# Half of a block's opening modulation as row products on the matrix engine, and attention maxima spread over the projections

## The chip, the cores and the metric

The kernel runs on one core of a Trainium2 chip. The time is the device time of one launch in microseconds, the median of several runs. The core's engines have queues of their own: TensorE (PE in the rows) multiplies, VectorE (DVE), ScalarE (ACT) and GpSimd (POOL) work element by element, and SyncE (SP) issues the transfers.

## What is computed

Two layers of a block with three mixers side by side (retention, latent attention, gated linear attention) on 1024 tokens of width 1024, all in fp32. Each layer is opened by a normalisation whose scale and shift come from a vector `c` (the modulation), and the projections of all mixers follow from its result:

```python
c_act = jax.nn.silu(c)
for l in range(DEPTH):
    shift, scale, gate = jnp.split(c_act @ ada_w[l] + ada_b[l], 3, axis=-1)
    h = rms_norm(x, norm_w[l]) * (1.0 + scale[:, None, :]) + shift[:, None, :]
    proj = h @ w_in[l]
    ...
    mixed = jnp.concatenate([r_o * jax.nn.silu(rz), m_o * jax.nn.silu(mz),
                             g_o * jax.nn.silu(gz)], axis=-1)
    x = x + gate[:, None, :] * (mixed @ w_out[l])
return rms_norm(x, final_norm)
```

`m_o` is softmax attention with 8 heads over 1024 queries and keys in causal blocks; its softmax subtracts a maximum of the scores, which the kernel has to find first.

## The kernel before

Everything is kept transposed: channels lie on the partitions, in 8 tiles of 128 channels by 1024 tokens, each in two halves of 512 tokens. Every product is made of three multiplications (`mm3`, L554 to L558): operands are split into a high part, rounded for the fast format, and a low part, and PE does high by high, high by low and low by high into one PSUM bank. The order on PE is the order in which the code is written; the other engines' orders are set by a scheduler that goes by estimated times, with some steps pinned.

**The opening** (`start`). Transfers are issued in order of need: the tiles of x, then for each of the 8 tiles the weights of the modulation, and between the first of them the weights of three projections (rq1, rq2, rk1). Modulation comes in columns of 128 channels: `column(k)` makes the scale of tile k as a product along the row on DVE (`along(1)`, L301: one pass over 1024 elements, the sum kept), and the shift on PE as 8 fp32 multiplications with one moving column each (L311) for the first `SHIFT_PE` = 5 columns, or by a second pass on DVE for the rest. `make(k)` makes tile k: scaling on DVE (L347), high part on ACT (L348), low part on DVE (L354), with the next column's work put between the two. Then `mm` multiplies tile k with each of three weights, 18 multiplications of 512 columns; the first three tiles defer some of them by the table `behind`, as the weights are split (`w_split`, a cast on ACT and a subtraction on DVE) only one by one.

**The maxima** (`mla_max`). For each head, eight query blocks of 128 are multiplied with all the keys that they see, up to 512 at a time (L1245, 12 multiplications a head, 96 a layer), and DVE reduces each (L1247). A head ends with a closing: a reduce over the blocks (L1213), a multiplication that turns the result round (L1217), a copy and a store. The function is a generator that runs as a task: `proj`, `proj_v` and others call `tick()` as they go, which counts every task down and runs it up to its next `yield`, whose number says how many ticks to pause. So `MAXW` = 1.15 ticks lie between two maxima, and a closing waits 7 ticks between its reduce and its multiplication, during which the head's other maxima wait too, as it is called inside with `yield from`. `drain(t)` runs a task to its end at once. In `layer` the task `big` starts before the projection gk, runs through gv (called pv in the rows), gz0, gz1, mz0 to mz3, and what is left of it is drained ahead of mv, the values of the latent attention, which starts in `mla_first` and `mla`. Also in these projections stand `next_chunk` calls: six pieces of modulation for this layer and the next, each 8 passes over 512 elements on DVE (L576), with pieces at c, g, k, n and so on (`CHUNKS`), and an addition (L579).

`self.maxp` names the PSUM pools that the maxima rotate through; two banks at a time.

Of the kernel before, what the change touches and what calls it, by code (L numbers as in the profile page):

```python
# [16 lines left out]
D = 1024  # L17
DEPTH = 2
# [17 lines left out]
SHIFT_PE = 5  # L36
MAXW = 1.15
# [77 lines left out]
def host_layout(x, c, positions, norm_w, ada_w, ada_b, w_in, mla_q_norm, w_uq, mla_kv_norm,  # L115
# [20 lines left out]
    A["aws"] = ada_w[0][:, :128 * SHIFT_PE].reshape(KT, 128, SHIFT_PE, 128).transpose(2, 1, 0, 3).reshape(SHIFT_PE, 128, D)  # L136
# [5 lines left out]
    def col(v):  # L142
# [5 lines left out]
        c[0].reshape(KT, 128).T], 1)  # L148
# [8 lines left out]
for _n, _w in (("normw", DEPTH * 8), ("adab", DEPTH * 24), ("qn", DEPTH * 2), ("kvn", DEPTH),  # L157
               ("gb2", DEPTH), ("gln", DEPTH), ("fin", 8), ("inv", 1), ("c", 8)):
    VO[_n] = _o
    _o += _w  # L160


class Builder:
# [55 lines left out]
    def start(self):  # L219
# [24 lines left out]
        for k in range(KT):  # L244
            if k < len(names):
                wst[names[k]] = self.sl(name="wst")
                dma(wst[names[k]], A["wi"][0, MIDX[names[k]]])
            aw[k] = [self.sl(name="aw") for _ in range(2)]
            dma(aw[k][1], A["awc"][2 + k // 4, k % 4])
            dma(aw[k][0], A["aws"][k] if k < SHIFT_PE else A["awc"][k // 4, k % 4])  # L250
# [10 lines left out]
        self.silu(self.silc, self.vec[:, o:o + KT], self.sm([128, KT]), self.sm([128, KT]))  # L261
        ab = self.sm([128, KT])
# [30 lines left out]
        def column(k):  # L293


            self.lab = "ada_"
            ch, j = k // 4, slice(k % 4, k % 4 + 1)
            t = self.sm([128, 2])

            def along(i):  # L300
                V.scalar_tensor_tensor(aw[k][i], aw[k][i], 1.0, self.silrow, ALU.mult, ALU.mult,  # L301
                                       accum_out=t[:, i:i + 1])
            along(1)
            o = VO["normw"] + k
            V.scalar_tensor_tensor(self.mod[0][2 + ch][:, j], t[:, 1:2], ab[:, k:k + 1], self.vec[:, o:o + 1],
                                   ALU.add, ALU.mult)
            src = t[:, 0:1]
            if k < SHIFT_PE:
                ps = self.ps()
                for i in range(KT):  # L310
                    nc.tensor.matmul(ps[:, 0:1], aw[k][0][:, 128 * i:128 * i + 128], self.silc[:, i:i + 1],  # L311
                                     start=(i == 0), stop=(i == KT - 1))
                src = ps[:, 0:1]
            else:
                along(0)
            o = VO["adab"] + k
            nc.scalar.activation(self.mod[0][ch][:, j], src, AF.Identity, bias=self.vec[:, o:o + 1])
        w_split("rq1")
# [19 lines left out]
        def make(k):  # L338
# [10 lines left out]
            if 0 < k < KT - 1:  # L349
                column(k + 1)  # L350
# [4 lines left out]
            if k == 0:  # L355
                column(1)
            return last
        behind = {0: (("rq1", 0),), 1: (("rq1", 1), ("rq2", 0), ("rq2", 1)),
                  2: (("rq1", 2), ("rq2", 2), ("rk1", 0), ("rk1", 1), ("rk1", 2))}
        for k in range(KT):  # L360
            self.start_last = make(k)
            if k < 2:
                w_split(names[k + 1])
            for n, i in behind.get(k, [(n, k) for n in names]):
                mm(n, i)
            if k == 2:
                self.trig(ang, kk, s)
# [827 lines left out]
    def mla_max(self, l):  # L1195
# [14 lines left out]
        def close(h, mx):  # L1210
# [3 lines left out]
            yield 7  # L1214
# [9 lines left out]
        for h in range(MH):  # L1224
            yield MAXW
# [6 lines left out]
            for i in range(8):  # L1232
                n = 128 * (i + 1)
                for j in range((n + 511) // 512):
                    if i or j:
                        yield MAXW
                    if i == 2 and done:
                        yield from close(*done)
                        done = None
                        yield MAXW  # L1240
# [228 lines left out]
    def layer(self, l, src):  # L1469
# [3 lines left out]
        self.maxp = ("mm", "s")  # L1473
# [48 lines left out]
        for i in range(2):  # L1522
            mixed[6 + i] = self.proj_silu(l, f"gz{i}")
            self.next_chunk("jk"[i])
        mz = [self.proj_silu(l, "mz0")]
# [63 lines left out]
```

## Time and profile before

| | |
|---|---|
| median of 3 runs | 1185.25 us (1184.59 to 1190.17) |
| the profiled execution | 1184.63 us, its span 1182.8 us |
| mean granted clock of PE | 0.977 of full speed |
| PE, DVE, ACT, POOL busy | 95%, 67%, 50%, 45% of the span |
| chain that ended last | PE 75%, DVE 12%, ACT 4%, DMA 4% |
| moved by DMA | 169 MB, mean 143 GB/s |

The profile is one execution on the chip. Busy time of an engine is that of its instructions; a matmul's end is modelled, so neighbouring ones overlap in their rows. The granted clock says at what share of 2.4 GHz the chip let PE run; 0.50 is 1.2 GHz. In a row of a timeline the first number is its start in us, the second its length, then engine, line, operation, names of the tiles (result, then operands), partitions and elements, and "x16" for a run of 16 records; brackets say how long the engine had waited just before and for whom.

### The profile page before, as it was taken

What the parts mean: (1) busy time and instruction counts of PE and PEld (TensorE: products, weight loads), DVE (VectorE), ACT (ScalarE), POOL (GpSimd) and SP (SyncE); (2) the same over time, 40 slices, a digit from 0 to 9 for tenths busy, and PEclk for the clock granted to TensorE, in tenths of its full rate; (3) what the DMA queues carried; (4) which work ended last, traced back from release to release, by engine and by line L of the source; (5) the groups of instructions that cost most, each with busy time, mean ns of one, the idle gap of its engine ahead of it and who ended that gap; (6) DMA issues with size and microseconds to landing.
All of it is one profiled execution on the core that took longest, in us unless ns stands there. A gap on an engine that the chain in (4) does not pass through costs nothing.

```text
span 1182.8 us, 16979 instructions
## 1 busy us (share of the span) xinstructions
PE 1128.0 (95%) x5968; PEld 942.6 (80%) x5968; DVE 796.7 (67%) x1366; ACT 596.6 (50%) x1164; POOL 529.5 (45%) x459
## 2 busy tenths in 40 slices
PE   6999999998999899999999999999899999999996
PEld 4878977787878688887887898778788868888896
DVE  7866595686675656768875476666675666686754
ACT  6434334433545578853543434434256447886431
POOL 0064153643443346673555333444553334668620
PEclk8899999998999899999999999999999989999998
DMA  9816563651136434248453356355111653424722
GB/s 370 296 48 194 170 225 133 187 170 41 42 120 201 119 90 108 64 152 302 169 183 99 99 172 238 99 184 157 41 41 41 195 134 90 108 63 163 249 88 72
DMA packets 65585, 169.01 MB, mean 143 GB/s; under 512 B 10262, under 2 KB 13334, under 8 KB 65500
## 3 DMA queue, kind: packets, MB, share of 16 engines
q1 hardware_dynamic: 65500, 167.93, 44.7%
q8 instruction: 47, 0.77, 0.3%
q14 instruction: 38, 0.31, 0.1%
HBM read 125.36 MB, written 38.41 MB: 138 GB/s over the span
## 4 chain that ended last, share of the span: by engine, by line
PE 75%; DVE 12%; ACT 4%; DMA 4%; issue 3%; POOL 1%; SPq 0%; DVEq 0%; ACTq 0%; POOLq 0%
PE mhead_psacc L1296 3%; PE mhead_psacc L1294 3%; PE mhead_psacc L1295 3%; PE wo_pspj L558 2%; PE wo_pspj L556 2%; PE wo_pspj L557 2%; PE pmz_pspj L556 2%; PE wo_pss L557 2%; PE wo_pss L556 2%; PE wo_pss L558 2%; PE pmz_pspj L557 2%; PE pmz_pspj L558 2%; DVE mmax_mx L1247 2%; PE mhead_pss L1263 2%; PE mhead_pss L1262 2%
## 5 line engine op out<-in xcount | busy, mean ns | idle before, releaser
L457 POOL TENSOR_TENSOR wwo_wl<-wwo_wst,wwo_wh 128x1024 fp32r<-128x1024 f32 x27 | 69.0, 2559 | 40.6 <-ACT wwo_wh L456 40.5
L1271 POOL TENSOR_TENSOR mhead_wh<-mhead_p,mhead_wh 128x384 fp32r<-128x384 f32 (+1 forms) x48 | 58.1, 1211 | 56.7 <-DVE mhead_wh L1270 56.7
L1247 DVE TENSOR_REDUCE mmax_mx<-mmax_psmm 128x1 f32<-128x512 f32 (+1 forms) x96 | 57.3, 596 | 26.4 <-PE mmax_psmm L1245 25.6
L576 DVE SCALAR_TENSOR_TENSOR ada_aw<-ada_aw,silrow 128x512 f32<-128x512 f32 x64 | 62.0, 986 | 18.5 <-DMA ada_aw<-awc 18.2
L1276 DVE TENSOR_TENSOR mhead_ph<-mhead_pss,mhead_ph 128x512 fp32r<-128x512 f32 x48 | 33.1, 689 | 38.6 <-ACT mhead_pss L1275 38.6
L556 PE MATMUL pmz_pspj<-mkh_h,wmz_wh 128*128 128x512 f32 x128 | 52.5, 410 | 0.0
L1271 POOL TENSOR_TENSOR mhead_wl<-mhead_p,mhead_wl 128x128 fp32r<-128x128 f32 (+1 forms) x48 | 35.8, 746 | 34.1 <-DVE mhead_wl L1270 34.1
L557 PE MATMUL pmz_pspj<-mkh_h,wmz_wh 128*128 128x512 f32 x128 | 50.3, 393 | 0.0
L558 PE MATMUL pmz_pspj<-mkh_h,wmz_wl 128*128 128x512 f32 x128 | 50.1, 392 | 0.0
L558 PE MATMUL wo_pspj<-gran_mx,wwo_wl 128*128 128x512 f32 (+1 forms) x120 | 44.8, 374 | 1.7 <-POOL wwo_wl L457 1.7
L556 PE MATMUL wo_pspj<-gran_mx,wwo_wh 128*128 128x512 f32 (+1 forms) x120 | 45.3, 377 | 0.2 <-ACT wwo_wh L456 0.2
L1245 PE MATMUL mmax_psmm<-mmax_mxk,mmax_mxq 104*128 104x512 f32 (+1 forms) x96 | 38.9, 408 | 6.6 <-DVE mmax_mx L1247 5.9
L557 PE MATMUL wo_pspj<-gran_mx,wwo_wh 128*128 128x512 f32 (+1 forms) x120 | 44.8, 373 | 0.0
L556 PE MATMUL wo_pss<-gran_mx,wwo_wh 128*128 128x512 f32 (+1 forms) x120 | 44.6, 371 | 0.0
L558 PE MATMUL wo_pss<-gran_mx,wwo_wl 128*128 128x512 f32 (+1 forms) x120 | 44.1, 368 | 0.0
L557 PE MATMUL wo_pss<-gran_mx,wwo_wh 128*128 128x512 f32 (+1 forms) x120 | 44.1, 368 | 0.0
L600 ACT ACTIVATE ssq_sq<-ssq_x 128x512 f32<-128x512 f32 (+1 forms) x31 | 16.5, 534 | 51.7 <-DVE ssq_x L1373 51.7
L457 POOL TENSOR_TENSOR wrk_wl<-wrk_wst,wrk_wh 128x1024 fp32r<-128x1024 f32 x3 | 8.1, 2688 | 76.0 <-ACT wrk_wh L456 76.0
L1247 DVE TENSOR_REDUCE mmax_mx<-mmax_pss 128x1 f32<-128x256 f32 (+2 forms) x72 | 36.5, 507 | 7.5 <-PE mmax_pss L1245 6.8
L605 DVE TENSOR_TENSOR ssq_sq<-ssq_sq,ssq_sq 128x512 f32<-128x512 f32 (+1 forms) x30 | 30.5, 1017 | 14.0 <-ACT ssq_sq L600 14.0
L556 PE MATMUL pv_pspj<-wgv_wh,mkh_h 128*128 128x256 f32 x128 | 38.5, 301 | 0.0
L1274 ACT ACTIVATE mhead_ph<-mhead_pss 128x512 fp32r<-128x512 f32 x48 | 28.6, 596 | 17.6 <-PE mhead_pss L1264 17.0
(565 smaller groups left out, 4140.6 us busy)
## 6 DMA issues: line engine op xcount, KB each, us to landing
ada_aw<-awc SPq DMA_DIRECT2D x64, 256.0 KB
wwo_wst<-wo SPq DMA_DIRECT2D x32, 512.0 KB
aw<-awc SPq DMA_DIRECT2D x11, 512.0 KB
x<-xT SPq DMA_DIRECT2D x8, 512.0 KB
kn<-mk_ph SPq DMA_DIRECT2D x16, 256.0 KB
kn<-mk_pl SPq DMA_DIRECT2D x16, 256.0 KB
qn<-mq_ph SPq DMA_DIRECT2D x16, 256.0 KB
qn<-mq_pl SPq DMA_DIRECT2D x16, 256.0 KB
```

The costliest lines, as they stand in the source:

```text
L457: (eng or nc.gpsimd).tensor_tensor(lo, src, hi.bitcast(F32), ALU.subtract)
L556: mm(ps, lh, rh, start=start, stop=False)
L557: mm(ps, lh, rl, start=False, stop=False)
L558: self.last = mm(ps, ll, rh, start=False, stop=stop)
L576: step = nc.vector.scalar_tensor_tensor(v, v, 1.0, self.silrow[:, cs], ALU.mult, ALU.mult, accum_out=t[:, 2 * j + i:2 * j + i + 1])
L1245: nc.tensor.matmul(ps[:, :w], st["q"][0:104, 128 * i:128 * i + 128], st["k"][0:104, 512 * j:512 * j + w], start=True, stop=True)
L1247: nc.vector.tensor_reduce(mx[:, i, j:j + 1], ps[:, :w], AX.X, ALU.max)
L1271: nc.gpsimd.tensor_tensor(pl, p, ph.bitcast(F32), ALU.subtract)
L1276: nc.vector.tensor_tensor(pl, s, ph.bitcast(F32), ALU.subtract)
L1294: mm(acc[:, o], vh, ph, start=(j == 0), stop=False, skip_group_check=True)
L1295: mm(acc[0:64, o], vl, ph, start=False, stop=False, skip_group_check=True)
L1296: mm(acc[:, o], vh, pl, start=False, stop=last, skip_group_check=True)
```

## The change

Two parts. In the opening, transfers put the three projections' weights first, then four pairs of columns (0 to 3), then eight tiles in another layout (`awk`) for the other four columns. Columns 1 to 3 have both of their products on DVE; only column 0 has its shift on PE. The columns 4 to 7 are made as two rows (channel groups 3, the scales, and 1, the shifts): `row` multiplies the vector, repeated to 32 columns (`silrep`), with 512 columns of weights, eight fp32 multiplications, spread over four groups of 32 columns of the array by `tile_position` so that four partial sums lie in one bank; `row_copy` brings them to SBUF on ACT, and `row_out` turns each 128 entries back into a column and adds the four partial sums with four small multiplications against a selecting vector. `row(3)` follows tile 1's multiplications on PE, `row(1)` tile 2's, `row_out(3)` precedes tile 3's, and `row_out(1)` follows them. All weights are split ahead of the first column, each tile issues its 18 multiplications at once, and the sines' table work (`trig`) goes one tile later.

In the maxima, the pause of 1.15 ticks becomes 1.45 up to the end of gz1 and 0.95 after it, and a head's closing becomes a task of its own, started at the next head's second block, with 6 ticks in between; the maxima go on meanwhile. `host_layout` adds `awk` and the selecting vector `sel`.

```diff
@@ -33,8 +33,7 @@
 LAG = 7
-SHIFT_PE = 5
-MAXW = 1.15
+MAXW = (1.45, 0.95)
 RW = (18, 6)
@@ -133,7 +132,8 @@
     A["wukv"] = np.concatenate([ukv[..., :64].reshape(L, 128, 512), ukv[..., 64:].reshape(L, 128, 512)], -1)
-    A["aws"] = ada_w[0][:, :128 * SHIFT_PE].reshape(KT, 128, SHIFT_PE, 128).transpose(2, 1, 0, 3).reshape(SHIFT_PE, 128, D)
+    A["aws"] = ada_w[0][:, :128].reshape(KT, 128, 128).transpose(1, 0, 2).reshape(128, D)
+    A["awk"] = ada_w[0].reshape(4, 2, 128, 6, 512)[:, :, :, 1:4:2].transpose(3, 0, 2, 1, 4).reshape(2, 4, 128, 1024)
     A["awc"] = ada_w.transpose(0, 2, 1).reshape(L * 6, 4, 128, D)
@@ -241,13 +241,17 @@
         wst, aw = {}, {}
-        for k in range(KT):
-            if k < len(names):
-                wst[names[k]] = self.sl(name="wst")
-                dma(wst[names[k]], A["wi"][0, MIDX[names[k]]])
+        for n in names:
+            wst[n] = self.sl(name="wst")
+            dma(wst[n], A["wi"][0, MIDX[n]])
+        for k in range(4):
             aw[k] = [self.sl(name="aw") for _ in range(2)]
-            dma(aw[k][1], A["awc"][2 + k // 4, k % 4])
-            dma(aw[k][0], A["aws"][k] if k < SHIFT_PE else A["awc"][k // 4, k % 4])
+            dma(aw[k][1], A["awc"][2, k])
+            dma(aw[k][0], A["awc"][0, k] if k else A["aws"])
+        for ch in (3, 1):
+            aw["row", ch] = [self.sl(name="aw") for _ in range(4)]
+            for i in range(4):
+                dma(aw["row", ch][i], A["awk"][ch // 2, i])
         self.ahead()
@@ -259,6 +263,8 @@
         self.silu(self.silc, self.vec[:, o:o + KT], self.sm([128, KT]), self.sm([128, KT]))
+        silrep = self.pt((128, KT, 32), name="silrep")
+        V.tensor_copy(silrep, self.silc.unsqueeze(2).to_broadcast([128, KT, 32]))
         ab = self.sm([128, KT])
@@ -305,7 +311,7 @@
             src = t[:, 0:1]
-            if k < SHIFT_PE:
+            if k == 0:
                 ps = self.ps()
@@ -315,7 +321,32 @@
             nc.scalar.activation(self.mod[0][ch][:, j], src, AF.Identity, bias=self.vec[:, o:o + 1])
-        w_split("rq1")
+
+        def row(ch):
+
+            self.lab = "ada_"
+            ps = self.ps()
+            for i in range(KT):
+                g = slice(32 * (i % 4), 32 * (i % 4) + 32)
+                nc.tensor.matmul(ps[g, :], silrep[:, i, :], aw["row", ch][i // 2][:, 512 * (i % 2):512 * (i % 2) + 512],
+                                 start=(i < 4), stop=(i >= 4), tile_position=(0, g.start))
+            return ps
+
+        def row_copy(ch):
+            r = self.pt(name="row")
+            nc.scalar.copy(r, rows[ch])
+            rows[ch] = r
+
+        def row_out(ch):
+
+            self.lab = "ada_"
+            ps, r = self.ps(), rows[ch]
+            for j in range(4):
+                nc.tensor.matmul(ps[:, j:j + 1], r[:, 128 * j:128 * j + 128], self.vcol("sel", 0),
+                                 start=(j == 0), stop=True, skip_group_check=True)
+            self.ada_out(0, ch, ps)
+        for n in names:
+            w_split(n)
         self.lab = "rstd_"
@@ -346,7 +377,7 @@
                 nc.scalar.activation(g[:, 0, :], ts[hf], AF.Identity, bias=b)
-            if 0 < k < KT - 1:
+            if 0 < k < 3:
                 column(k + 1)
@@ -355,15 +386,23 @@
             return last
-        behind = {0: (("rq1", 0),), 1: (("rq1", 1), ("rq2", 0), ("rq2", 1)),
-                  2: (("rq1", 2), ("rq2", 2), ("rk1", 0), ("rk1", 1), ("rk1", 2))}
+        rows = {}
         for k in range(KT):
             self.start_last = make(k)
-            if k < 2:
-                w_split(names[k + 1])
-            for n, i in behind.get(k, [(n, k) for n in names]):
-                mm(n, i)
             if k == 2:
+                row_copy(3)
+            if k == 3:
+                row_copy(1)
+                row_out(3)
+            for n in names:
+                mm(n, k)
+            if k == 1:
+                rows[3] = row(3)
+            if k == 2:
+                rows[1] = row(1)
+            if k == 3:
+                row_out(1)
+            if k == 3:
                 self.trig(ang, kk, s)
@@ -1211,7 +1250,7 @@
             nc.vector.tensor_reduce(m8, mx, AX.X, ALU.max)
-            yield 7
+            yield 6
             self.lab = "mmax_"
@@ -1222,7 +1261,7 @@
         for h in range(MH):
-            yield MAXW
+            yield self.maxw
             st = sets[h % 2]
@@ -1233,11 +1272,10 @@
                     if i or j:
-                        yield MAXW
-                    if i == 2 and done:
-                        yield from close(*done)
+                        yield self.maxw
+                    if i == 1 and done:
+                        self.task(close(*done))
                         done = None
-                        yield MAXW
                     self.lab = "mmax_"
@@ -1470,7 +1508,7 @@
         mixed = [None] * 8
-        self.maxp = ("mm", "s")
+        self.maxp, self.maxw = ("mm", "s"), MAXW[0]
         if l > 0:
@@ -1522,6 +1560,7 @@
             self.next_chunk("jk"[i])
+        self.maxw = MAXW[1]
         mz = [self.proj_silu(l, "mz0")]
...
         self.maxp = ("mm", "s")
```

On PE in the opening before, after tile 1's multiplications (`mkh_h` is a tile's high and low parts, `ada_wh` and `ada_wl` the weights' parts, L311 the column of tile 3):

```order
L556 MATMUL ada_pss_302<-mkh_h_347,ada_wh_332 128x512
L557 MATMUL ada_pss_302<-mkh_h_347,ada_wh_332 128x512
L558 MATMUL ada_pss_302<-mkh_h_347,ada_wl_333 128x512
L311 MATMUL ada_psmm_398<-silc,aw_163 128x1 x8
L556 MATMUL ada_pspj_299<-mkh_h_389,ssq_wh_272 128x512
L557 MATMUL ada_pspj_299<-mkh_h_389,ssq_wh_272 128x512
```

And with the change, from the end of tile 1 to tile 2 (L331 the row, `aw_167` to `aw_170` its weights):

```order
L596 MATMUL ada_psacc_314<-mkh_h_357,ada_wh_282 128x512
L597 MATMUL ada_psacc_314<-mkh_h_357,ada_wl_283 128x512
L331 MATMUL ada_psmm_385<-aw_167,silrep_200 32x512 x2
L331 MATMUL ada_psmm_385<-aw_168,silrep_200 32x512 x2
L331 MATMUL ada_psmm_385<-aw_169,silrep_200 32x512 x2
L331 MATMUL ada_psmm_385<-aw_170,silrep_200 32x512 x2
L595 MATMUL ada_pspj_309<-mkh_h_396,ssq_wh_274 128x512
L596 MATMUL ada_pspj_309<-mkh_h_396,ssq_wh_274 128x512
```

Where a column of eight one-column multiplications stood, a row of eight with 512 columns stands.

On DVE with the change, from tile 3's low parts to tile 4's scaling (`mod_90` and `mod_88` are the scales and shifts of columns 4 to 7, each made from a `row_out`):

```order
L385 SCALAR_TENSOR_TENSOR mkh_h_440<-mkh_ht_438,mod_87,mkh_h_440 128x512
L385 SCALAR_TENSOR_TENSOR mkh_h_443<-mkh_ht_439,mod_87,mkh_h_443 128x512
L625 TENSOR_TENSOR mod_90<-ada_psmm_450,vec 128x4
L628 SCALAR_TENSOR_TENSOR mod_90<-mod_90,vec 128x4
L625 TENSOR_TENSOR mod_88<-ada_psmm_475,vec 128x4
L378 SCALAR_TENSOR_TENSOR mkh_ht_486<-x_130,mod_90,rstd_y_286 128x512
L378 SCALAR_TENSOR_TENSOR mkh_ht_487<-x_130,mod_90,rstd_y_287 128x512
```

The shifts' addition stands ahead of tile 4's scaling, and it reads the `row_out` that follows all of tile 3's multiplications on PE.

On PE after mz3 before, where `drain(big)` runs (maxima L1245, a closing's multiplication L1217):

```order
L1245 MATMUL mmax_pss_3830<-mmax_mxk_2241,mmax_mxq_2240 128x384
L1245 MATMUL mmax_psmm_3833<-mmax_mxk_2241,mmax_mxq_2240 128x512
L1245 MATMUL mmax_pss_3836<-mmax_mxk_2241,mmax_mxq_2240 128x512
L1245 MATMUL mmax_psmm_3841<-mmax_mxk_2243,mmax_mxq_2242 128x128
L1245 MATMUL mmax_pss_3844<-mmax_mxk_2243,mmax_mxq_2242 128x256
L1217 MATMUL mmax_psmm_3849<-cst,mmax_sm_3847 8x128
L1245 MATMUL mmax_psmm_3854<-mmax_mxk_2243,mmax_mxq_2242 128x384
```

With the change, the maxima stand among the projections up to mz3; in mz0 of the first layer:

```order
L597 MATMUL pmz_pspj_3278<-mkh_h_544,wmz_wl_2937 128x512
L1283 MATMUL mmax_psacc_3320<-mmax_mxk_2226,mmax_mxq_2225 128x256
L595 MATMUL pmz_pspj_3278<-mkh_h_572,wmz_wh_2936 128x512
L596 MATMUL pmz_pspj_3278<-mkh_h_572,wmz_wh_2936 128x512
L597 MATMUL pmz_pspj_3278<-mkh_h_572,wmz_wl_2937 128x512
L1283 MATMUL mmax_psmm_3326<-mmax_mxk_2226,mmax_mxq_2225 128x512
L1256 MATMUL mmax_psmm_3329<-cst,mmax_sm_3291 8x128
L595 MATMUL pmz_pspj_3343<-mkh_h_324,wmz_wh_2936 128x512
```

None stands alone any more; nearly every three multiplications of a projection have one maximum behind them, and a closing stands right behind a maximum.

On DVE with the change, in the same place (L615 steps of a modulation piece, L1285 the reduces, L1252 the closing's reduce that the closing's multiplication above reads):

```order
L615 SCALAR_TENSOR_TENSOR ada_aw_3250,ada_sm_3243<-ada_aw_3250,silrow 128x512
L1285 TENSOR_REDUCE mmax_mx_3210<-mmax_psmm_3302 128x1
L490 SCALAR_TENSOR_TENSOR hnorm_sm_3226<-hnorm_sm_3224,hnorm_sm_3226 128x8
L1285 TENSOR_REDUCE mmax_mx_3210<-mmax_psacc_3308 128x1
L1285 TENSOR_REDUCE mmax_mx_3210<-mmax_psmm_3314 128x1
L1285 TENSOR_REDUCE mmax_mx_3210<-mmax_psacc_3320 128x1
L615 SCALAR_TENSOR_TENSOR ada_aw_3253,ada_sm_3243<-ada_aw_3253,silrow 128x512
L491 SCALAR_TENSOR_TENSOR hnorm_sm_3225<-hnorm_sm_3226,hnorm_sm_3225 128x8
L1252 TENSOR_REDUCE mmax_sm_3291<-mmax_mx_2865 128x8
L1285 TENSOR_REDUCE mmax_mx_3210<-mmax_psmm_3326 128x1
```

The closing's reduce is behind a step of the modulation, and ahead of the reduce of the maximum that PE multiplies just before.

## Rows read from the trace of the kernel before

**Rows 1.** The page: busy time of each engine in us, its share of the span, instructions.
```profile
PE 1128.0 (95%) x5968; PEld 942.6 (80%) x5968; DVE 796.7 (67%) x1366; ACT 596.6 (50%) x1164; POOL 529.5 (45%) x459
```

**Rows 2.** The page: the chain of work that ended last, by engine.
```profile
PE 75%; DVE 12%; ACT 4%; DMA 4%; issue 3%; POOL 1%; SPq 0%; DVEq 0%; ACTq 0%; POOLq 0%
```

**Rows 3.** Busy time by stretch, opening; last three columns granted clock, DMA share, GB/s.
```profile
26.10:35.50 9.40, 9.40 (x32) 8.14 (x32) 8.63 (x15) 3.72 (x6) 0.00 (x0) 0.50 1.03 420
...
48.30:70.40 22.10, 21.28 (x93) 16.84 (x93) 17.19 (x30) 9.65 (x18) 0.94 (x1) 1.00 0.48 143
```

**Rows 4.** The same view: stretch, length, PE, PEld, DVE, ACT, POOL busy; later stretches.
```profile
252.00:280.30 28.30, 24.90 (x172) 22.99 (x171) 24.54 (x45) 9.00 (x20) 12.15 (x15) 0.90 0.23 66
...
333.60:364.10 30.50, 28.84 (x137) 23.00 (x136) 26.02 (x52) 14.34 (x27) 12.37 (x9) 1.00 0.56 178
391.30:403.10 11.80, 8.96 (x27) 5.41 (x26) 10.18 (x23) 3.38 (x6) 3.63 (x7) 0.76 0.72 181
897.80:928.20 30.40, 30.40 (x150) 25.01 (x150) 18.50 (x35) 15.69 (x28) 11.17 (x9) 1.00 0.41 119
955.40:967.20 11.80, 8.97 (x27) 5.42 (x26) 10.18 (x23) 3.38 (x6) 5.44 (x10) 0.72 0.75 164
```

**Rows 5.** PE's waits after the opening: us in total, times, longest.
```profile
PE mmax_psmm L1245 <- DVE mmax_mx L1247: 5.9, 6, 2.3
...
PE glac_psacc L1009 <- DVE mmax_mx L1247: 3.4, 2, 1.7
```

**Rows 6.** Timeline of PE in the opening.
```profile
19.00 1.92 PE L311 MATMUL ada_psmm<-silc,aw 128*128 128x1 f32 x16
...
26.77 0.63 PE L557 MATMUL ada_pspj<-mkh_h,ssq_wh 128*128 128x512 f32 x1
...
28.90 3.41 PE L311 MATMUL ada_psmm<-silc,aw 128*128 128x1 f32 x16
...
70.14 0.39 PE L558 MATMUL ada_psacc<-mkh_h,mkh_wl 128*128 128x512 f32 x1
```

**Rows 7.** Timeline of DVE and ACT in the opening.
```profile
24.62 1.62 DVE L354 SCALAR_TENSOR_TENSOR mkh_h<-mkh_ht,mod,mkh_h 128x512 fp32r<-128x512 f32 x2
...
48.89 1.34 ACT L348 ACTIVATE mkh_h<-mkh_ht,mod 128x512 fp32r<-128x512 f32 x2
...
51.05 1.41 DVE L354 SCALAR_TENSOR_TENSOR mkh_h<-mkh_ht,mod,mkh_h 128x512 fp32r<-128x512 f32 x2
52.38 1.42 DVE L347 SCALAR_TENSOR_TENSOR mkh_ht<-x,mod,rstd_y 128x512 f32<-128x512 f32 x2
53.70 1.23 DVE L301 SCALAR_TENSOR_TENSOR aw<-aw,silrow 128x1024 f32<-128x1024 f32 x1
...
56.25 1.41 DVE L354 SCALAR_TENSOR_TENSOR mkh_h<-mkh_ht,mod,mkh_h 128x512 fp32r<-128x512 f32 x2
```

**Rows 8.** Timeline of PE: fp32 multiplications of 512 columns for the sum of squares.
```profile
13.68 5.42 PE L281 MATMUL psacc<-ssq_sq,ones 128*128 128x512 f32 x12 [3.36 <-DVE ssq_sq L280]
```

**Rows 9.** Timeline of PE: maxima alone, and the values behind them (mv).
```profile
391.38 0.34 PE L1245 MATMUL mmax_psmm<-mmax_mxk,mmax_mxq 104*128 104x384 f32 x1
...
403.03 0.41 PE L556 MATMUL mv_pspj<-wukvv_wh,pmz_lat 128*128 128x256 f32 x1
...
404.31 0.29 PE L556 MATMUL mv_pspj<-wukvv_wh,pmz_lat 128*128 128x256 f32 x1
...
970.84 0.33 PE L556 MATMUL mv_pspj<-wukvv_wh,pmz_lat 128*128 128x256 f32 x1
```

**Rows 10.** Timeline of PE: a maximum that waits in pv, and pv behind it.
```profile
275.87 0.48 PE L1245 MATMUL mmax_psmm<-mmax_mxk,mmax_mxq 104*128 104x128 f32 x1 [2.33 <-DVE mmax_mx L1247]
276.14 0.53 PE L556 MATMUL pv_pspj<-wgv_wh,mkh_h 128*128 128x256 f32 x1
```

**Rows 11.** The page's groups: the reduces, x96 of their 192; busy and mean ns, idle before.
```profile
L1247 DVE TENSOR_REDUCE mmax_mx<-mmax_psmm 128x1 f32<-128x512 f32 (+1 forms) x96 | 57.3, 596 | 26.4 <-PE mmax_psmm L1245 25.6
```

**Rows 12.** Groups of DVE in 334 to 364: the modulation's steps.
```profile
L576 DVE SCALAR_TENSOR_TENSOR ada_aw<-ada_aw,silrow 128x512 f32<-128x512 f32 x8 | 8.0, 1015 | 0.9 <-DMA ada_aw<-awc 0.9
```

More of the change, by code (lines that the diff above doesn't have):

```diff
@@ L147, in host_layout @@
         np.concatenate([gla_norm, gla_norm], 1).T, final_norm.reshape(KT, 128).T, INV,
-        c[0].reshape(KT, 128).T], 1)
+        c[0].reshape(KT, 128).T, (np.arange(128) % 32 == 0)[:, None].astype(f)], 1)
     A["cst"] = CST
@@ L157 @@
 for _n, _w in (("normw", DEPTH * 8), ("adab", DEPTH * 24), ("qn", DEPTH * 2), ("kvn", DEPTH),
-               ("gb2", DEPTH), ("gln", DEPTH), ("fin", 8), ("inv", 1), ("c", 8)):
+               ("gb2", DEPTH), ("gln", DEPTH), ("fin", 8), ("inv", 1), ("c", 8), ("sel", 1)):
     VO[_n] = _o
```

## Prediction

> **What bounds the kernel now.** I read the busy shares first: PE is busy 95% of the span [rows 1] and has 75% of the chain that ended last [rows 2], so time is won only where PE stands idle or runs at the lower clock, or where it does less. The table of stretches then says where that is. In the opening, 26.10 to 35.50, PE is busy all the time but at a granted clock of 0.50 (1.2 GHz), with DMA at 1.03 and 420 GB/s [rows 3]: a stretch bound by transfers and by PE's clock. From 48.30 to 70.40 PE is at 1.00 and busy 21.28 of 22.10 us [rows 3]: 93 records, 0.229 us each. The two stretches with maxima alone, 391.30 to 403.10 and 955.40 to 967.20, have PE busy 8.96 of 11.80 us at 0.76 and 0.72, and DVE busy 10.18 [rows 4]: DVE's reduces bound them. The stretch that holds pv, 252.00 to 280.30, leaves PE idle 3.40 us at a mean clock of 0.90 [rows 4]; the table of waits names the reduce for it, 5.9 us in 6 waits and 3.4 in 2 [rows 5].
>
> **The opening, step by step.** The sum is made against the profiled execution, 1184.63 us, which is 0.62 under the median of 1185.25.
>
> *Transfers.* Column 0's two weights now land behind all three weights of the projections instead of behind one. Two tiles of 512 KB at 420 GB/s [rows 3] are 1.25 us each: 2.5 us later. Before, the column's matmuls start at 19.00, when its weights are there [rows 6]; all that hangs on it moves to 2.5 later, DVE's first low parts among it, which were done at 24.62 + 1.62 = 26.24 [rows 7]. Now 28.7, I take 28.5, as nothing else on PE stands ahead of them.
>
> *PE's columns.* Four of five columns leave PE, 1.92 us for 16 records at full clock and 3.41 at half [rows 6]. The second multiplication of tile 0 was at 26.77 and the spacing at half clock is (28.90 - 26.77)/5 = 0.426 [rows 6]. Now the second is at 27.75 (the first half's low part), and the 17 that are left of tile 0 end by 27.75 + 17 x 0.426 = 35.0.
>
> *DVE's turn.* Columns 1 to 3 now cost two passes over 1024 instead of one. Such a turn exists before: from one tile's low parts at 51.05 to the next's at 56.25 it takes 5.20 us [rows 7]. For tile 1 two more passes lie in between (column 1's, ahead of the tile), so from 28.5 on: four passes of 1.23, two scalings of 1.42 together and half of the low parts, 0.7, are 7.0, with the small steps 7.3 [rows 7]. Tile 1's first low part is there at 35.8, 0.8 after PE has run dry.
>
> *PE after that.* 144 multiplications less 19 are 125, at 0.229 us 28.6, to 64.4. To it come two rows, two `row_out` of four one-column matmuls (half of 1.92 us, 0.95 each [rows 6]), and a stall at tile 4: DVE's last `ada_out` waits for the second `row_out`, which stands on PE behind all of tile 3. When it is done PE has nothing, and waits for the addition (0.2), the scaling (0.71 [rows 7]), ACT's high part (1.34/2 = 0.67 [rows 7]) and most of the low part (0.7): 2.6 us with the small gaps.
>
> *A row's price* has no row before. Eight fp32 matmuls with 512 columns: a record of the sum of squares of the same shape takes 5.42/12 = 0.43 to 0.45 us, two records a matmul, 0.86 [rows 8]. If the four column groups of the array work at once, a row is 2 x 0.86 = 1.7 us; if they run one after another, 8 x 0.86 = 6.9; and that at half clock 13.8. I take 2.3, near the lower end, since the columns of the four groups are disjoint and nothing in the code orders them. The Trainium skill (TensorE: Matmul & The Clock Gate, Part 3, The mechanism) says that a load of weights overlaps running matmuls only where the row group differs, which would speak against it, as here all four share every row; the same page's Measured speedup gives 2.38 times for three column tiles of 32, by which a row would be an estimated 2.9 us and the sum 1.2 us higher. No row of this kernel shows either.
>
> End of the opening: 64.4 + 4.6 + 1.9 + 2.6 = 73.5, against 70.14 + 0.39 = 70.5 [rows 6]: **+3.0 us**.
>
> **The maxima.** Asking 1.45 per maximum until the projections gz are done and 0.95 after, and closing a head as a task beside the next head instead of pausing 7 ticks, leaves no maxima for after mz3. Before, 22 of a layer's 96 ran there alone, from 391.38 to 403.03 [rows 9], 11.65 us; the second layer's stretch is as long [rows 4]. Their PE work, 8832 columns, 17.25 times 512, still has to be done among the projections: 17.25 x 0.229 = 3.95. That leaves a gain of 7.7 in each layer. Behind it mv's multiplications ran at half clock, to 404.31 and 970.84 [rows 9], which costs 0.6 and 1.4 us that go too. **-8.3 and -9.1.**
>
> *pv.* The slower rate before gz takes pressure from this stretch: 3.4 us idle and, at a mean clock of 0.90 over 28.3 us, 2.8 us by the clock [rows 4]; the single waits are as long as 2.33 us, and the multiplications behind it are at the lower clock, 0.53 us for 256 columns [rows 10]. The maxima in it stay nearly as many (27 after 26, by the order of the program), so I take half, **-3 per layer**, -6. At most it is all, -12, at least nothing.
>
> *What is late next.* gz: more maxima in it (22 for 15), and the chain of gla's values waited for a reduce for 1.7 us already [rows 5]: +1 per layer. mz0 and mz1 take 34 maxima for 21, 13 x 0.596 = 7.7 us of DVE [rows 11]. In the first layer DVE is busy 26.02 of 30.50 there [rows 4], with 8 steps of the modulation of 1.015 us [rows 12]: 33.8 us of DVE against 28.84 + 13 x 0.229 = 31.8 of PE. It is past PE by 2.0; and DVE's order puts a closing's reduce behind such a step while PE has the closing's matmul right behind the next maximum, so PE waits for DVE twice or more, about 1 us each: I take +4.5. In the second layer DVE has 18.50 + 7.7 of 30.40 [rows 4]: +0.5. mv now follows mz3 at once, beside its silu: +1 per layer. Together **+9**. Below, these could be nothing.
>
> **Sum.** 3.0 - 17.4 - 6 + 9 = -11.4; 1184.63 - 11.4 = **1173.2**, I write 1173.0.
>
> **The rivals.** About half a per cent, 5.9 us, is what a measurement of this kernel can tell from no change: faster is under 1179.3, slower over 1191.2.
>
> *The column groups run one after another at 2.4 GHz.* For it: nothing in the trace shows that pieces of the array work side by side. Against: PE needs only as much time as it needs, no order is asked for. Price: 2 x (6.9 - 2.3) = +9.2, **1182.4**. The rule of the Trainium skill named above (the same page and section) would lead there. 13%.
>
> *They run one after another at half clock (the other side).* The first row stands where PE has just waited for tile 1 and tile 2, and the clock before 35.5 was 0.50 in spite of PE being busy [rows 3]; if the waits keep it there, a row is 13.8 us, +23, **1196.2**, slower. It decides from some 11.4 us a row (18 us above my sum). Against: before, the clock rose in spite of waits of this size. 5%.
>
> *The block's stall only moves.* DVE's reduces still have two banks and PE still queues a projection's matmuls behind a maximum; if half of the 7.7 is lost again in each layer, it is +7.7, **1180.9**, no change. For it: the first layer's DVE in mz0 and mz1 [rows 4]. Against: mz2 and mz3 and the second layer have room. 14%.
>
> *All smooth.* pv's waits go wholly, -6 more, and mz0 and mz1 keep DVE just under PE, -3.5: **1163.7**. For it: the lower rate is what DVE's reduces ask for in pv. 13%.
>
> **How the numbers follow.** Forecast 55%, the rivals 13, 5, 14 and 13. Of the forecast two points fall within half a per cent, of the stall that moves nine of 14, of the groups one after another at full clock nine within and one above. Faster 0.53 + 0.13 + 0.05 + 0.03 = 0.74, same 0.20, slower 0.06. The range reaches from the smooth case to the groups in turn, 1163.0 to 1182.5: half of each of these two and the half-clock case lie outside.
>
> **What would show it.** Right: the last multiplication of the opening ends at 73 to 74, each group of eight row matmuls takes 1.7 to 3 us, PE idles 2 to 3 us ahead of tile 4; no stretch after mz3 holds maxima alone, and mv starts about 10 us sooner after mz3. PE's waits for reduces in pv are half of 3.4 us, and new ones of 1 us stand in mz0 and mz1 of the first layer. Wrong: rows of 7 us or more; a sum of waits for the reduce larger than before; or pv's clock as low as before. A mean granted clock well above 0.977 would mean that more went than I took.

## The result and the profile after

The changed kernel takes 1174.85 us (median of 7 runs) against 1186.81 of the kernel before, a ratio of 0.9917 with a 95% interval of 0.9891 to 0.9944: **faster by 0.8%**, as forecast (1173.0). The profiled execution takes 1174.35 us. Its page, for [rows 1]:

```profile
span 1172.5 us, 16921 instructions
PE 1115.8 (95%) x5952; PEld 932.3 (80%) x5952; DVE 790.4 (67%) x1358; ACT 596.5 (51%) x1162; POOL 527.4 (45%) x459
```

Where the 10.3 us of span came from shows in the time from a projection's first multiplication on PE to the next one's (from the timelines of PE; a second layer's stretch behind the first's):

| stretch | before | after | change | forecast, the prediction's terms put where they belong |
|---|---|---|---|---|
| opening, to the projection prk | 70.36 | 74.35 | +4.0 | +3.0 |
| prk to pgk | 159.52, 193.13 | 159.51, 193.29 | 0.0, +0.2 | 0 |
| pgk and pv | 50.43, 48.87 | 47.85, 45.20 | -2.6, -3.7 | -3, -3 |
| gz | 53.34, 51.16 | 51.40, 51.39 | -1.9, +0.2 | +1, +1 |
| mz0 to mv (with the maxima alone) | 69.38, 67.22 | 63.56, 59.52 | -5.8, -7.7 | -3.2, -7.2 |
| mv to the next layer or the end | 203.73, 215.66 | 208.43, 218.00 | +4.7, +2.3 | +0.4, -0.4 |

The sum was right to 1.1 us by the profiles (-10.3 for -11.4); three of its terms were not. Busy time by stretch after the change (columns as in [rows 3, 4]; the first two lie in the opening, then come pv, gz, mz0 with most of mz1, and the start of mv; the last two are the second layer's mz0 with most of mz1, and mv):

```profile
26.10:35.50 9.40, 7.17 (x19) 4.99 (x18) 9.09 (x17) 2.65 (x5) 0.00 (x0) 0.64 1.02 420
55.70:60.20 4.50, 4.20 (x10) 3.11 (x11) 4.37 (x7) 2.01 (x3) 0.00 (x0) 0.62 0.93 261
247.59:281.71 34.12, 31.88 (x222) 28.87 (x220) 30.35 (x61) 11.59 (x24) 13.79 (x15) 0.95 0.35 114
281.71:333.11 51.40, 50.57 (x288) 42.98 (x287) 34.93 (x85) 27.02 (x73) 23.17 (x31) 1.00 0.15 43
333.11:363.70 30.59, 28.41 (x130) 22.54 (x129) 25.79 (x59) 13.93 (x27) 10.50 (x9) 0.94 0.51 145
396.67:406.00 9.33, 5.73 (x31) 5.22 (x30) 3.06 (x6) 5.48 (x10) 5.46 (x10) 0.82 1.01 224
895.00:925.50 30.50, 30.50 (x148) 24.51 (x146) 23.82 (x46) 14.76 (x28) 11.31 (x10) 1.00 0.43 127
954.50:964.00 9.50, 5.90 (x32) 5.23 (x31) 3.42 (x6) 6.14 (x11) 5.46 (x10) 0.86 0.94 222
```

No stretch of maxima alone is left; in its place PE is busy 5.73 of 9.33 us at the start of mv. The table of PE's waits names the new one; the two waits for reduces of [rows 5] are down from 5.9 and 3.4 us to 1.6 and 1.7:

```profile
PE mv_pspj L595 <- DVE pmz_vl L1230: 7.2, 2, 3.6
...
PE glac_psmm L1010 <- DVE mmax_mx L1285: 1.7, 4, 0.5
PE mmax_psmm L1283 <- DVE mmax_mx L1285: 1.6, 3, 0.7
PE mmax_psmm L1256 <- DVE mmax_sm L1252: 1.5, 1, 1.5
```

The opening on PE, for [rows 6]: the two rows, the second `row_out`, tile 4's first three multiplications and the last of all.

```profile
39.92 1.92 PE L331 MATMUL ada_psmm<-aw,silrep 128*32 128x512 f32 x16
...
46.12 1.92 PE L331 MATMUL ada_psmm<-aw,silrep 128*32 128x512 f32 x16
...
53.10 0.95 PE L345 MATMUL ada_psmm<-vec,mkh_row 128*128 128x1 f32 x8
55.71 0.49 PE L595 MATMUL ada_pspj<-mkh_h,ssq_wh 128*128 128x512 f32 x1 [1.67 <-ACT mkh_h L379]
56.50 0.60 PE L596 MATMUL ada_pspj<-mkh_h,ssq_wh 128*128 128x512 f32 x1 [0.29 <-DVE mkh_h L385]
56.89 0.63 PE L597 MATMUL ada_pspj<-mkh_h,ssq_wl 128*128 128x512 f32 x1
...
74.12 0.39 PE L597 MATMUL ada_psacc<-mkh_h,ada_wl 128*128 128x512 f32 x1
```

A row takes 1.92 us, near the lower end. Ahead of tile 4 PE waits 1.67 and 0.29 us, and then the multiplications from 56.89 to 59.88 start 0.43 us apart instead of 0.23: the granted clock there is 0.50, that is 1.2 GHz.

### The profile page after: what moved, and what is told of

Its sections match the earlier page's. It is cut to its first block, busy times and chain, and to the rows that moved or that the text cites. A ratio compares the mean times of both kernels' runs of the same rounds, so it can differ in the third digit from the quotient of the medians.

```text
span 1172.5 us, 16921 instructions
## 1 busy us (share of the span) xinstructions
PE 1115.8 (95%) x5952; PEld 932.3 (80%) x5952; DVE 790.4 (67%) x1358; ACT 596.5 (51%) x1162; POOL 527.4 (45%) x459
## 4 chain that ended last, share of the span: by engine, by line
PE 76%; DVE 12%; DMA 4%; ACT 4%; issue 3%; POOL 1%; SPq 0%; DVEq 0%; ACTq 0%; POOLq 0%
PE mhead_psacc L1334 3%; PE mhead_psacc L1332 3%; PE mhead_psacc L1333 3%; PE pmz_pspj L595 3%; PE pmz_pspj L596 2%; PE pmz_pspj L597 2%; PE wo_pss L595 2%; PE wo_pss L596 2%; PE wo_pss L597 2%; PE wo_pspj L595 2%; PE wo_pspj L597 2%; PE wo_pspj L596 2%; PE mhead_pss L1301 2%; PE mhead_pss L1300 2%; PE mhead_pss L1302 2%
## 5 line engine op out<-in xcount | busy, mean ns | idle before, releaser
L1285 DVE TENSOR_REDUCE mmax_mx<-mmax_psmm 128x1 f32<-128x512 f32 (+1 forms) x96 | 57.4, 598 | 25.5 <-PE mmax_psmm L1283 24.0
L615 DVE SCALAR_TENSOR_TENSOR ada_aw<-ada_aw,silrow 128x512 f32<-128x512 f32 x64 | 61.6, 985 | 16.9 <-DMA ada_aw<-awc 16.5
L1309 POOL TENSOR_TENSOR mhead_wl<-mhead_p,mhead_wl 128x128 fp32r<-128x128 f32 (+1 forms) x48 | 35.8, 746 | 33.0 <-DVE mhead_wl L1308 33.0
L595 PE MATMUL pv_pspj<-wgv_wh,mkh_h 128*128 128x256 f32 x128 | 37.7, 295 | 0.0
L596 PE MATMUL pv_pspj<-wgv_wl,mkh_h 128*128 128x256 f32 x128 | 36.7, 287 | 0.0
L597 PE MATMUL pv_pspj<-wgv_wh,mkh_h 128*128 128x256 f32 x128 | 36.7, 287 | 0.0
```

What stands on the lines that cost most here:

```text
L595: mm(ps, lh, rh, start=start, stop=False)
L596: mm(ps, lh, rl, start=False, stop=False)
L597: self.last = mm(ps, ll, rh, start=False, stop=stop)
L615: step = nc.vector.scalar_tensor_tensor(v, v, 1.0, self.silrow[:, cs], ALU.mult, ALU.mult, accum_out=t[:, 2 * j + i:2 * j + i + 1])
L1285: nc.vector.tensor_reduce(mx[:, i, j:j + 1], ps[:, :w], AX.X, ALU.max)
L1309: nc.gpsimd.tensor_tensor(pl, p, ph.bitcast(F32), ALU.subtract)
```

## The experiments

**Which part gives, which takes.** The maxima alone in the kernel before (the changed lines of `MAXW` and `maxw`, `close` and `task`), and the opening alone (the same lines undone in the changed kernel).

> The opening of the kernel before with the maxima of the changed one. If the two parts add up, the 4.0 us that the changed kernel's opening lost (its last multiplication ends at 74.51 instead of 70.53) come back: a span of 1172.5 - 4.0 = 1168.5, that is 14.3 under the kernel before, with mv waiting 3.6 us for DVE in each layer as in the changed kernel. Rival: the later opening helped the maxima (other alignment of transfers and weights), and the gain is under 11 us, a span over 1171.5.

> The changed opening with the maxima of the kernel before. If the parts add up: span 1182.8 + 4.0 = 1186.8, the last multiplication of the opening at 74.1, and the two stretches with maxima alone of 11.65 us each are back. Rival (the opening's loss is taken up later by work that was waiting anyway): within 1 us of the kernel before.

Measured: maxima alone 1170.72 us, ratio 0.9873 [0.9839, 0.9907], span 1168.4 (expected 1168.5). Opening alone 1192.12 us, ratio 1.0058 [1.0037, 1.0079], span 1187.7 (expected 1186.8). By the times the parts add up: 0.9873 x 1.0058 is 0.993, the whole change 0.9917 [0.9891, 0.9944]. The opening by itself is a loss of 0.6%, its rival falls. That the spans came out so close is in part luck. With the opening alone the last multiplication of the opening started at 72.44 instead of the 74.1 expected, and 2.3 us of the longer span lie in the second layer's gz, which the edit doesn't touch; with the maxima alone the opening gave back 1.7 us and not 4.0.

The opening's end is not the same in every execution: prk starts at 70.36 and 72.66 with the opening of before (before, maxima alone), and at 74.35, 72.67, 72.74, 74.32, 75.39 and 72.78 with the changed one (six profiles of kernels that share it). The wait of 1.67 us is in all six; in the three of them that end before 73, the opening alone among them, tile 4's multiplications run on at full clock.

**The price of a row.**

```diff
-                g = slice(32 * (i % 4), 32 * (i % 4) + 32)
+                g = slice(0, 32)
...
-                                 start=(i < 4), stop=(i >= 4), tile_position=(0, g.start))
+                                 start=(i == 0), stop=(i == KT - 1), tile_position=(0, g.start))
...
```

> All eight multiplications of a row in one group of 32 columns, one partial sum instead of four; the first 32 partitions alone are copied. If the 1.92 us of a row come from four groups of columns working at once, a row now takes 8 x 0.86 = 6.9 us, and the span grows by up to 2 x 5 = 10 us, to 1182.5. Rival: 32 stationary columns make a multiplication cheap by themselves, and a row stays at about 1.9 us, with the span at 1172.5.

```profile
40.26 7.05 PE L331 MATMUL ada_psmm<-aw,silrep 128*32 128x512 f32 x16
```

7.05 us for the same eight multiplications (PE's timeline of that kernel), 1185.64 us in all, ratio 0.9998 [0.9978, 1.0018]: four groups at once are what makes the row cheap, and without it the whole gain is gone. (The lines left out copy and add up 32 partitions instead of 128.) The opening grew by 11.7 us, the span by 7.4, to 1179.9, since pgk and pv, mz0 to mv and the stretch behind it took 4.2 us less in that execution.

**The stall ahead of tile 4.**

```diff
             for n in names:
                 mm(n, k)
+                if k == 3 and n == names[0]:
+                    row_out(1)
...
-            if k == 3:
-                row_out(1)
```

> The second row_out stands behind the first six of tile 3's multiplications instead of behind all 18. If DVE's addition for the shifts, which stands ahead of tile 4's scaling, is what PE waited for, both waits ahead of tile 4 (1.67 and 0.29 us) go, and with them the ten multiplications at half clock behind them (about 8.5 x 0.2 = 1.7): the opening ends 3.6 us sooner, at 70.9, and the span is 1168.9. If the half clock has another cause than the wait, 2.0 us sooner only: 1170.5. Rival: the row's copy on ACT is not there in time, so that PE waits inside tile 3 instead, and nothing is won.

```profile
50.13 0.95 PE L345 MATMUL ada_psmm<-vec,mkh_row 128*128 128x1 f32 x8
...
54.22 0.49 PE L595 MATMUL ada_pspj<-mkh_h,ssq_wh 128*128 128x512 f32 x1 [0.30 <-ACT mkh_h L379]
55.01 0.50 PE L596 MATMUL ada_pspj<-mkh_h,ssq_wh 128*128 128x512 f32 x1 [0.29 <-DVE mkh_h L385]
55.35 0.40 PE L597 MATMUL ada_pspj<-mkh_h,ssq_wl 128*128 128x512 f32 x1
```

The wait falls to 0.30 and 0.29, the multiplications behind it stay 0.23 us apart, and prk starts at 71.28, 3.1 us sooner. The time is 1171.01 us, ratio 0.9877 [0.9851, 0.9903]; the interval overlaps that of the changed kernel by a little. Yet the span of the profiled execution, the slowest of the six, is 1172.2 where 1168.9 was expected: pgk and pv took 51.66 us instead of 47.85. There, PE waited 1.71 us for a reduce, which stood behind one step of the modulation on DVE, which ran beside POOL's making of a low part (rows of PE, DVE and POOL); and the granted clock of the stretch was 0.93 instead of 0.96.

```profile
249.81 0.39 PE L1283 MATMUL mmax_pss<-mmax_mxk,mmax_mxq 104*128 104x256 f32 x1 [1.71 <-DVE mmax_mx L1285]
...
246.76 2.39 DVE L615 SCALAR_TENSOR_TENSOR ada_aw<-ada_aw,silrow 128x512 f32<-128x512 f32 x1
...
246.12 2.48 POOL L496 TENSOR_TENSOR wgz_wl<-wgz_wst,wgz_wh 128x1024 fp32r<-128x1024 f32 x1 [4.61 <-ACT wgz_wh L495]
```

**mv's wait.** ACT and PE of the changed kernel behind mz3:

```profile
396.87 0.59 ACT L756 COPY pmz_mz<-pmz_pspj 128x512 f32<-128x512 f32 x1 [0.41 <-PE pmz_pspj L597]
397.49 0.63 ACT L469 ACTIVATE pmz_zt<-pmz_mz 128x512 f32<-128x512 f32 x1
...
400.20 0.63 ACT L473 ACTIVATE pmz_zu<-pmz_zu 128x512 f32<-128x512 f32 x1 [0.76 <-DVE pmz_zu L472]
400.74 1.05 ACT L1229 CAST pmz_vh<-mv_pspj 128x512 fp32r<-128x512 f32 x2
```

```profile
398.21 0.28 PE L597 MATMUL mv_pspj<-wukvv_wh,pmz_lat 128*128 128x256 f32 x1
402.08 0.58 PE L595 MATMUL mv_pspj<-wukvv_wh,pmz_lat 128*128 128x256 f32 x1 [3.60 <-DVE pmz_vl L1230]
402.46 0.41 PE L596 MATMUL mv_pspj<-wukvv_wl,pmz_lat 128*128 128x256 f32 x1
```

mv's two banks are full at 398.5; the copy that has to read them first stands on ACT behind the silu of mz3's last half until 400.74, and DVE's low part (`pmz_vl`) follows the copy. Before, the maxima alone lay over that silu (ACT's steps from 392.20 to 396.96, the maxima to 403.03). Two ways to take the wait away:

```diff
-            ps = self.ps("pj", (128, 2, 256))
+            ps = self.ps(("pj", "acc")[t // 4] if g == 0 else "pj", (128, 2, 256))
```

> The changed kernel with the first half of the values (mv) in four PSUM banks instead of two (two of them from the pool that the attention uses right after). If PE's wait of 3.6 us in each layer is for a bank that ACT's copies free too late, behind the silu of mz3, PE goes on through all 24 multiplications (2.9 us) and the next scores; the wait shrinks to about 1 us: 2.5 us less per layer and less half clock behind it, a span of 1172.5 - 5 to 6 = 1167. Rival: ACT's queue itself is what is late, since the next scores' exponentials and the values need it as well, and PE's wait moves from mv to the attention's first multiplications: gain under 1.5 us in all.

Measured: 1172.37 us, ratio 0.9883 [0.986, 0.9907]. PE's wait moved to the attention's first product, as the rival said; mv to the next layer or the end took 205.29 and 219.18 us, 3.1 less and 1.2 more than in the changed kernel:

```profile
PE mhead_psacc L1332 <- DVE pmz_vl L1230: 5.4, 2, 2.7
```

The other puts that silu behind mv (`late` is the call of `silu` for mz3's second half, made in `mla` once the first scores are issued):

```diff
-            self.silu(v, v, self.pt(name="zt"), self.pt(name="zu"), self.nc.gpsimd)
+            late = lambda: self.silu(v, v, self.pt(name="zt"), self.pt(name="zu"), self.nc.gpsimd)
+            if (name, hf) == ("mz3", 1):
+                self.late = late
+            else:
+                late()
...
```

> The changed kernel with the silu of mz3's second half put behind mv's first copies and the next scores. If PE's 3.6 us behind mv is ACT's queue (the five ACT steps of that silu and DVE's step between them stand ahead of mv's copies), the wait falls to the 0.7 us or so of the kernel before, in both layers: 6 us less, a span of 1166.5. Rival: the silu's steps are then in the way of the attention's exponentials, and the stretch from mv to the next layer is as long as before: gain under 2 us.

```profile
397.67 0.58 ACT L1233 CAST pmz_vh<-mv_pspj 128x512 fp32r<-128x512 f32 x1
...
403.63 0.63 ACT L469 ACTIVATE pmz_zt<-pmz_mz 128x512 f32<-128x512 f32 x1
```

```profile
399.03 0.39 PE L595 MATMUL mv_pspj<-wukvv_wh,pmz_lat 128*128 128x256 f32 x1 [0.46 <-DVE pmz_vl L1234]
```

1165.24 us, ratio 0.9834 [0.9808, 0.9861], span 1163.1 (expected 1166.5). The wait is 0.46 us, and mv to the next layer or the end takes 203.03 and 213.64 us, 5.4 and 4.4 less than in the changed kernel. The half clock behind the wait went with it: the granted clock was 0.50 from 402.00 to 404.80 in the changed kernel, and is 1.00 from 396.50 to 401.50 here. So ACT's queue was the cause; the bank was only where it showed.

**What empties the stretch after mz3, and what the rates do.** The closing inside the loop again (`yield from close` at the third block, 7 ticks), and the old rate (`MAXW = (1.15, 1.15)`) with closings as tasks.

> The changed kernel with a head's closing called inside the loop again (at the third block, 7 ticks), the new rates kept. If the closing as a task is what empties the block after mz3, 22 maxima are left there again and cost 11.65 us per layer; without the 3.6 us of mv's wait, and with the lower rate in pv kept: span 1172.5 + 2 x (7.7 + 1 - 3) = 1184, nearly the kernel before. Rival (the rates are what empties it): span within 2 us of 1172.5.

> The changed kernel with the old rate, 1.15 ticks throughout, closings as tasks. If the rates are worth what the table of stretches shows for pv, about 2.4 and 3.7 us, and the lower rate late costs little: span 1172.5 + 5 = 1177.5, with PE idle 2 to 3 us in pv for DVE's reduces. Rival: pv's idle time comes from single slow steps on DVE that happen to meet a split on POOL (one step of 2.39 us instead of 0.69 was behind a wait of 1.7 in another run), not from the rate: span within 2 us of 1172.5.

With the closing inside, 1183.34 us (0.997 [0.9954, 0.9986], span 1180.7), and DVE bounds the stretch again (the view of stretches, that kernel):

```profile
393.00:406.00 13.00, 10.30 (x32) 6.88 (x33) 11.38 (x25) 2.95 (x6) 3.33 (x8) 0.69 0.93 200
```

So the closing as a task removes it, the rates do not. With the old rate, 1178.11 us (0.9944 [0.9925, 0.9963], which overlaps the changed kernel's interval); its profile, of the fastest of the nine executions, has a span of 1172.7. pgk and pv take 48.22 and 47.38 us (changed: 47.85, 45.20), gz 54.49 and 54.45 (51.40, 51.39), mz0 to mv 59.02 and 56.55 (63.56, 59.52). The rates mostly move maxima, and time with them: pgk and pv, gz, and mz0 to mz3 hold 34, 28 and 34 of a layer's 96 with the old rate, 27, 22 and 47 with the new one (26, 15 and 55 before, with those alone). The 5 us that I expected back in pv are 2.6, and in the first layer 0.4. PE's waits of that kernel:

```profile
PE glac_psacc L1048 <- DVE mmax_mx L1285: 4.4, 4, 1.6
...
PE mmax_psmm L1256 <- DVE mmax_sm L1252: 2.4, 1, 2.4
```

**Repairs together.** The early `row_out` with mv's banks, and with the late silu; the latter with `MAXW = (1.45, 1.1)`; and with gz0's low part made by DVE:

> The second row_out behind six of tile 3's multiplications, and mv in four banks. If both repairs hold and add up: the opening 3 us shorter and mv's waits 5 us less than in the changed kernel: a span of 1164 to 1165 where pv meets no slow step, 1168 where it does as in the run with the early row_out alone. Rival: as with the banks alone, under 1.5 us from them: 1168 to 1171.

> The second row_out early and mz3's silu late together. If both repairs hold: 3 us from the opening and 6 from mv against the changed kernel, less the 4 us that pv lost in both profiles with the early row_out: a span of 1166 to 1168, and 1163.5 in executions without the slow step in pv. If the late silu costs what it saves: 1171 to 1172.

> The same with 1.1 ticks between maxima after gz instead of 0.95. The old rate of 1.15 throughout had the stretch from mz0 to mv 4.5 and 3.0 us shorter than the changed kernel, but gz 3 us longer each. If the maxima are too dense for DVE in mz0 and mz1, 1.1 wins 2 to 4 us in the first layer and 1 to 3 in the second, without loss in gz: a span 4 us under that of the kernel with both repairs. Rival: the shorter stretch with the old rate only shows the maxima that it placed in gz (a few fewer were left for mz), and nothing is won.

> Both repairs, and the low part of gz0's weights made by DVE instead of POOL. With the early row_out, pgk and pv took 51.7 and 51.9 us in the first layer, 46.4 to 48 elsewhere; in them a modulation step on DVE took 2.39 us instead of 0.69 while POOL made this low part (2.48 us). If POOL's work is what slows the step, pgk and pv now take 46.5 to 48.5 us in the first layer. Rival: DVE is late there because its data land late (it waited 2.39 us for them), and the 1.23 us of the low part come on top: 51 to 53 us.

| kernel | us | ratio | span | pgk and pv |
|---|---|---|---|---|
| early, banks | 1171.01 | 0.9877 [0.9846, 0.9908] | 1174.1 | 51.86, 45.21 |
| early, late silu | 1161.93 | 0.9810 [0.9791, 0.9829] | 1159.2 | 46.49, 45.21 |
| the same, 1.1 ticks | 1160.50 | 0.9810 [0.9786, 0.9834] | 1158.7 | 46.38, 45.22 |
| the same as the second, gz0 split on DVE | 1162.16 | 0.9808 [0.9786, 0.9830] | 1161.6 | 46.05, 45.27 |

With the two repairs the changed kernel is 1.9% faster than the kernel before, where it was 0.8% without; the span of 1159.2 is 4 us under the lowest that was expected. mv's banks add nothing to the early `row_out` alone, which had 1171.01 us as well, and their span, with a slow step in pv, is 3 us above the highest expected. The rate of 1.1 gains 0.5 us in each layer's mz by the profiles (62.85 and 59.04 against 63.43 and 59.52) and nothing that the times can tell: the rival. The last run doesn't decide its question, since with POOL's split in place its partner had no step over 0.79 us beside it either.

Read side by side, the profiles with the changed maxima show what pgk and pv of the first layer hang on: one of the eight steps of the modulation on DVE, the one beside POOL's split. (An earlier one, of 1.77 us, is the same in all.) In seven of them, the one without that split included, it took 0.69 to 1.03 us and the stretch 46.05 to 46.65; in the changed kernel 1.36 and 47.85; in the two with the early `row_out`, by itself and with mv's banks, 2.39 and 2.38, and 51.66 and 51.86.

## Why the prediction was right, and where it was not

**Right in the whole and in its places.** The maxima alone were worth what they lasted less PE's own work: the second layer's mz0 to mv lost 7.7 us for 7.2 forecast. The opening lost time, for the reasons given: the second multiplication at 27.89 (27.75 said), tile 1's first low part ends at 35.8, the row 1.92 (2.3), the stall of tile 4 1.96 us (2.6). pv gained 2.6 and 3.7 (3). The last multiplication ended at 74.51, half a microsecond behind the 73 to 74 said, and the mean granted clock rose to 0.984. Of the rivals, rows in turn and rows at half clock were excluded by the row's 1.92 us: four groups take 1.92 us, one 7.05, 3.7 times. The rule of the Trainium skill (TensorE: Matmul & The Clock Gate, Part 3, The mechanism) that a load of weights overlaps running matmuls only where the row group differs, which would have led to rows in turn, cost at most 0.2 us here (1.92 us a row, where 1.7 was the lower end). The Trainium skill (the same page, Part 3, Measured speedup), with 2.38 times for three column tiles, points the same way as the trace; no run here has three. The stall that only moves was half right: 7.2 us of wait came back, but at mv and from ACT's queue, not from DVE's reduces. All smooth, at 1163.7, did not come.

**Wrong: "mv now follows mz3 at once, beside its silu: +1 per layer".** I named the silu and priced it at 1 us; it stood ahead of mv's copies in ACT's queue, and PE waited 3.60 us, with half clock behind it. With the clock that was to come back (-0.6, -1.4) the stretch was to change by +0.4 and -0.4 us, and it took +4.7 and +2.3. Moving the silu gave 5.4 and 4.4 back: the wait was priced at less than a third of what it lasted, and the clock behind it at nothing.

**Mis-sized: the "+4.5" for mz0 and mz1 of the first layer.** The wait stands where it was seen in the order, a closing's multiplication on PE for a closing's reduce on DVE:

```profile
342.94 0.39 PE L1256 MATMUL mmax_psmm<-cst,mmax_sm 128*8 128x128 f32 x2 [1.47 <-DVE mmax_sm L1252]
```

But the gain against before was only 1.9 us smaller than in the second layer (-5.8 and -7.7), not 4: the first layer's stretch had been 2.2 us the longer one before as well (69.38 and 67.22), and I did not take that off. From mz0's first multiplication to mz2's took 36.07 us after 30.49; 13 more maxima at 0.229 us are 3.0 of the 5.6, which leaves 2.6 for the 4.5.

**Mis-sized: gz "+1 per layer".** It was -1.9 and +0.2: the chain's wait for a reduce went from 1.7 us at most to 0.5 (0.8 in all in each layer), and the first layer's granted clock from 0.96 to 1.00.

**Right in size, half wrong in cause: pv "by the slower rate".** The old rate with the new closing already has 2.2 of the first layer's 2.6 us and 1.5 of the second's 3.7, with 34 maxima in the stretch: the closing did that. The new rate, which leaves 27, adds 2.2 in the second layer. What it adds in the first is not settled: both profiles have a slow step there (1.58 us with the old rate, 1.36 in the changed kernel), and with steps of 1.03 us or less the stretch was some 1.8 us under the old rate's 48.22. I also read too much into [rows 5]: the 3.4 us lie in gz, 1.7 in each layer. In pgk and pv PE waited 3.9 and 3.4 us for reduces before, and 1.1 in each layer now.

**Missed in the opening:** the half clock behind the stall at tile 4, 1.7 us, in three profiles of six. The opening's cost is 0 to 5 us from profile to profile (2.3 between the lowest of each kind); by the times of the opening alone it is 0.6% [0.4, 0.8], which is 7 us and more than the profiles place in the opening. Where the rest of it lies stays open. So errors of +7 (mv) and +1 (opening) met errors of -4 (gz) and -3 (mz): that the total was better than its terms was luck.

## What to carry to other kernels

When a stretch that only one engine bounds is taken out, ask what else ran under it: here a silu on ACT, hidden by the maxima, became PE's longest wait. When a result is needed a whole tile later, put the small step that makes it inside the work before, not behind it. Compare the parts of a change apart: here one part paid for the other.

## What the runs showed of the hardware

A step on DVE with both inputs in SBUF waited for POOL's running subtraction, and its record shows that as a long step: 0.69 us alone, 2.39 and 2.38 in the two profiles with the slowest step, 1.36 in the changed kernel. The second of these two, with the early `row_out` and mv's banks, DVE and POOL:

```profile
247.19 2.38 DVE L615 SCALAR_TENSOR_TENSOR ada_aw<-ada_aw,silrow 128x512 f32<-128x512 f32 x1
...
246.36 2.67 POOL L496 TENSOR_TENSOR wgz_wl<-wgz_wst,wgz_wh 128x1024 fp32r<-128x1024 f32 x1 [4.60 <-ACT wgz_wh L495]
```

In both, DVE's step ends some 0.55 us after POOL's (249.15 after 248.60, 249.57 after 249.03), whenever it began. It is the same throughout the changed kernel's trace: all nine steps of the modulation that began while POOL worked on two tiles took 1.16 to 2.88 us and ended 0.55 or 0.56 us after POOL, and 27 reduces of 512 columns that began so took 0.68 or 0.69, as they do alone; they read PSUM. The Trainium skill (SBUF — State Buffer, SBUF: two separate sides) says that a DVE instruction with two SBUF inputs and a GpSimd one that reads SBUF share a port pair, which whichever starts first holds for its whole length; these rows agree. Why the step met the subtraction early in two of the profiles is open: in the one with the early `row_out` alone, DVE had waited 2.39 us for the data of the step before it, 0.70 in the changed kernel.

The same wait of 1.67 us in the opening was followed by a granted clock of 0.50 in the changed kernel's profile (56.89 to 59.88) and by 1.00 with the opening alone (55.65 to 60.20); what decides was not found.
